# Two weight strips of the next product are loaded and split before the attention half ends, and the strips' buffers become two stores of two

## The chip, the core and the metric

The kernel runs on one core of a Trainium2 chip. A core has a matrix engine (TensorE, "PE" in the rows below; its weight loads are a row of their own, "PEld"), a vector engine (VectorE, "DVE"), a scalar engine (ScalarE, "ACT"), a general engine (GpSimd, "POOL") and a queue engine that here only issues loads (SyncE, "SP"). Each works through its own list of instructions, and they wait for each other by semaphores. The metric is the time of one execution on the device in microseconds, the median of several.

## What is computed

Two layers of an encoder over 256 tokens of width 2048, in float32. Cut to what matters:

```python
for l in range(2):
    u = rmsnorm(x, norm_mix[l])
    proj = u @ w_in[l]                       # 2048 x 8256: queries, keys, values, gates
    y_a = mla_attention(...) @ w_o_mla[l]    # 8 heads, 1024 x 2048
    y_b = neighbourhood_attention(...) @ w_o_na[l]
    merged = sigmoid(gate_a) * y_a + sigmoid(gate_b) * y_b
    x = x + merged @ w_out[l]                # 2048 x 2048
    h = rmsnorm(x, norm_mlp[l]) @ w_ff1[l]   # 2048 x 8192
    x = x + square(relu(h)) @ w_ff2[l]       # 8192 x 2048
return rmsnorm(x, norm_final)
```

## The kernel before

**Products in three pieces.** A float32 number is split into a rounded part `hi` and a remainder `lo`, and a product is made of three matmuls: hi times hi, lo of the activations times hi of the weights, hi of the activations times lo of the weights. So every piece of weights goes through three steps: a load into a buffer `raw` (1 MB, three such buffers, issued by SP), a cast by ACT that makes `hi`, and a subtraction by DVE that makes `lo`. These are the lines L176 and L177 in `parts` for the large products, and L197 and L198 in `weights` for the others. A matmul (L537) takes one 128 x 128 block of the activations as stationary operand (from a tile called `pair`) and 512 columns of a `hi` or `lo` strip as moving operand; it adds into one of eight PSUM banks.

**Two halves of a layer.** The attention half (half A) makes the projections, the two attentions and their output products; the last of them multiplies by `w_o_mla`, in four column blocks (`for c4 in range(4)`, matmuls at L306 and L310). Behind each block `merge` (L902, L903) gates and adds the two attention results, and `turned` (transposes at L605, splits at L165 and L169) turns the sum into stationary tiles for the next product. The second half (half B) makes the product by `w_out` and then the MLP, all with `gemm_s`.

**gemm_s.** One call makes 1024 columns of a product over 2048 rows. It goes through eight double rows of weights in the order 0, 4, 1, 5, 2, 6, 3, 7. Three of them are in `pairs` and are done with one level of Strassen's scheme, which needs seven block products in place of eight: DVE first makes four sums of weight blocks (L574, L577, L578), then `cut` splits 1536 columns of the raw weights and 2048 columns of sums. The other five double rows are split whole (2048 columns, a "whole strip"). At the end the eight banks are combined (L587 on ACT, L586 on DVE) and handed to `evac`. For `w_out` this adds to the residual (L936) and starts `turned_pair`: transposes (L507), a scaled copy by ACT (L926 behind `w_out`, L980 behind `w_ff1`), sums of activations (L473 to L476), a cast by ACT (L516) and a subtraction by DVE (L517).

**Buffers.** Half A and half B hold pools of their own, opened and closed at the border. In half B the split strips lie in `wpool2` with four buffers for `hi` and four for `lo`; each holds up to 2048 columns, and a new strip takes one of the four that has come free. In half A the pool `wpool` holds strips of 1024 columns, and `tmp` holds the temporaries of the attention heads.

**Order.** The program is written as if in one stream; generators started with a lag (`start`, advanced by `tick` after every few matmuls) put transposes and splits between the matmuls. A scheduler then sets the order of the instructions on each engine, going by costs of its own. On the chip each engine keeps to that order: a cast that stands behind another one on ACT waits for it, even when its own data is there.

Of the kernel before, what the change touches and what calls it, by code (L numbers as in the profile page):

```python
# [39 lines left out]
P = 128  # L40
# [35 lines left out]
def trunk(ctx: ExitStack, tc: tile.TileContext, x, x_turned, w_in, w_uq, w_ukv, rpb, w_o_mla, w_o_na,  # L76
# [7 lines left out]

    tmp = wpool = None
    hbufs, smalls, strips = HBUFS, SMALL, False

    def bank():
        return psum.tile([P, 512], F32, tag="bank", name="bank", bufs=8)
# [81 lines left out]

    def parts(src):

        lo, hi = (wpool.tile([P, 2048 if strips else 1024], F32R, tag=tag, name=tag,
                             bufs=hbufs)[:, :src.shape[-1]] for tag in ("lo", "hi"))
        nc.scalar.copy(hi, src)  # L176
        nc.vector.tensor_tensor(lo, src, hi.bitcast(F32), op=ALU.subtract)  # L177
        return hi, lo
# [342 lines left out]
        return  # L521
        yield

    def gemm_s(w, c0, get, order, pairs, evac):

# [17 lines left out]
            for i, ah, al, wh, wl in todo:  # L545
                mm(i, ah, wl)

        def cut(src):
            out, step = [], 2048 if strips else 1024
            for c in range(0, src.shape[-1], step):  # L550
                hi, lo = parts(src[:, c:min(c + step, src.shape[-1])])
                out += [(hi[:, i:i + 512], lo[:, i:i + 512]) for i in range(0, hi.shape[-1], 512)]
            return out

        first = next(j for j in order if j in pairs)
        for j in order:
            raw = raws.tile([P, 2048], F32, tag="raw", name="raw", bufs=RBUFS)
            nc.sync.dma_start(raw.rearrange("p (k n) -> p k n", n=1024),
                              w[2 * j * P:(2 * j + 2) * P, c0:c0 + 1024].rearrange("(k p) n -> p k n", p=P))
            if j not in pairs:  # L560
                ws = cut(raw)
                ah, al = get(j)
                products(*((i, ah[2 * k + t], al[2 * k + t], *ws[2 * k + side])
                           for k in range(2) for i, t, side in ((2, 0, 1), (3, 0, 0), (4, 1, 1), (8, 1, 0))))
                continue
            if j == first:
                drain()
            if strips:
                whole_ts = wpool.tile([P, 2048], F32, tag="sums", name="sums", bufs=1)
                ts = whole_ts[:, :1024], whole_ts[:, 1024:]  # L570
            else:
                ts = [tmp.tile([P, 1024], F32, tag="pp", name="sums", bufs=2) for _ in range(2)]
            t1, t3, t2, t4 = (s[:, i:i + 512] for s in ts for i in range(0, 1024, 512))
            nc.vector.tensor_tensor(ts[0].rearrange("p (a n) -> p a n", a=2),  # L574
                                    raw[:, :512].rearrange("p (a n) -> p a n", a=1).to_broadcast([P, 2, 512]),
                                    raw[:, 512:1536].rearrange("p (a n) -> p a n", a=2), op=ALU.subtract)
            nc.vector.tensor_tensor(t2, raw[:, 1024:1536], t1, op=ALU.subtract)  # L577
            final = nc.vector.tensor_tensor(t4, raw[:, 1536:], t2, op=ALU.subtract)  # L578
            with tc.issue_after(final.ins):
                w11, w22, w21 = cut(raw[:, 512:])  # L580
            w1, w3, w2, w4 = cut(whole_ts) if strips else cut(ts[0]) + cut(ts[1])
            (a11, _, a12, a22, s1, s2, s3, s4), (l11, _, l12, l22, r1, r2, r3, r4) = get(j)
            products((1, a11, l11, *w11), (2, a12, l12, *w21), (3, s4, r4, *w22), (5, s1, r1, *w1),
                     (7, s3, r3, *w3), (6, s2, r2, *w2), (4, a22, l22, *w4))
# [167 lines left out]
    for l in range(DEPTH):  # L752
        half_a = ExitStack()
        hbufs, smalls, strips = HBUFS, SMALL, False
        wpool = half_a.enter_context(tc.tile_pool(name="wpool", bufs=4, reuse_waits="tile"))
        tmp = half_a.enter_context(tc.tile_pool(name="tmp", bufs=2, reuse_waits="tile"))
        wi = w_in[l]
        mix = norm

# [136 lines left out]
        local(2)  # L896
        local(3)
        mg, ms4, mf4 = [None] * NC, [None] * (NC // 2), [None] * (NC // 2)
        for c4 in range(4):
            def merge(t, ps):  # L900
                m, h = part[t, c4], other[t, c4]
                nc.vector.scalar_tensor_tensor(h, h, 1.0, ps, op0=ALU.add, op1=ALU.mult)  # L902
                nc.vector.tensor_tensor(m, m, h, op=ALU.add)  # L903
                if t == 1:
                    start(turned(lambda t, c4=c4: part[t, c4], c4, mg, lambda c: 0.5, mf4, MERGED), 4)

            gemm_a(w_o_mla[l], c4 * 512, att, merge)
            if c4 == 2:
                start(forms(mf4, MERGED, ms4), 4)
        half_a.close()  # L910


        last = l == DEPTH - 1
        half_b = ExitStack()
        strips = True
        wpool = half_b.enter_context(tc.tile_pool(name="wpool2", bufs=4, reuse_waits="tile"))
        tmp = half_b.enter_context(tc.tile_pool(name="tmp2", bufs=2, reuse_waits="tile"))
        mlp = RowNorm()
        xg = [None] * (NC // 2)

# [9 lines left out]
        for g in range(2):  # L930
# [8 lines left out]
                        start(turned_pair(lambda t, c4=c4: xt[t][:, c4 * 512:(c4 + 1) * 512], c, xg, 2 * c4 + c,  # L939
                                          2 * c4 + c in FIRST, gained(2 * c4 + c)), 4)  # L940

            gemm_s(w_out[l], g * 1024, blocks(mg, ms4, MERGED), ORDER, MERGED, residual)
        mlp.scale()

        norm = RowNorm()
# [139 lines left out]
```

## Time and profile before

| | |
|---|---|
| median of three executions | 2600.32 us (2599.18 to 2600.32) |
| profiled execution | 2599.52 us, of which the profile's span is 2597.7 us |
| granted TensorE clock | 0.999 |
| PE busy | 2585.0 us |
| DVE busy | 2176.4 us |
| ACT busy | 1487.5 us |

The profile has a page with one row per engine and groups of instructions by line, and views of the trace: a timeline of one engine (start, duration, engine, line, operation, output and inputs, and in square brackets how long the engine had been idle before and whose work ended that), sums of the waits by what was waited for, and the chain of work that ended last. The rows that carry the argument stand with the prediction.

### The profile page before, as it was taken

How to read it: one execution, taken by the hardware profiler on the slowest of the kernel's cores; microseconds unless marked ns; L12 is line 12 of the kernel's file. 1: busy time of each engine (PE TensorE's matmuls, PEld its weight loads, DVE VectorE, ACT ScalarE, POOL GpSimd, SP SyncE). 2: the span in 40 equal slices, each digit the busy share in tenths (PEclk: the TensorE clock that was granted, in tenths of full speed). 3: DMA queues.
4: the chain of work that ended last, by engine and by line, in shares of the span. 5: the costliest groups of instructions: out<-in, count | busy, mean ns of one | idle time of the engine just before them, and what ended most of it. 6: DMA issues, size and time to landing. Idle time of an engine off the chain costs nothing.

```text
span 2597.7 us, 32260 instructions
## 1 busy us (share of the span) xinstructions
PE 2585.0 (100%) x12432; PEld 2171.9 (84%) x12432; DVE 2176.4 (84%) x2538; ACT 1487.5 (57%) x1732; POOL 98.0 (4%) x118
## 2 busy tenths in 40 slices
PE   9999999999999999999999999999999999999998
PEld 8888889888888888888888888898888888888887
DVE  7778889699988898888667788896999988988885
ACT  6555557456655645546545555574666556555463
POOL 0200000000000010000001000000000000100000
PEclk9999999999999999999999999999999999999999
DMA  7655564555577585675565555645656765856754
GB/s 266 217 171 195 180 205 151 165 191 195 195 219 220 176 259 198 202 239 171 178 201 178 173 194 182 205 149 161 197 180 211 234 199 192 246 194 209 243 180 145
DMA packets 173994, 511.06 MB, mean 197 GB/s; under 512 B 13840, under 2 KB 18832, under 8 KB 173584
## 3 DMA queue, kind: packets, MB, share of 16 engines
q1 hardware_dynamic: 164640, 491.78, 57.1%
q0 software_dynamic: 8768, 16.78, 3.3%
q8 instruction: 97, 1.59, 0.2%
q10 hardware_dynamic: 432, 0.43, 0.1%
q14 instruction: 57, 0.47, 0.1%
HBM read 494.28 MB, written 2.10 MB: 191 GB/s over the span
## 4 chain that ended last, share of the span: by engine, by line
PE 99%; issue 0%; ACT 0%; DVE 0%; POOL 0%; DVEq 0%; POOLq 0%; ACTq 0%
PE bank L537 67%; PE bank L306 8%; PE bank L354 6%; PE bank L310 4%; PE bank L359 3%; PE bank L285 2%; PE bank L507 1%; PE bank L260 1%; PE bank L286 1%; PE bank L314 1%; PE bank L316 1%; PE bank L315 1%; PE bank L258 1%; PE bank L669 1%; PE bank L605 0%
## 5 line engine op out<-in xcount | busy, mean ns | idle before, releaser
L537 PE MATMUL bank<-hi,pair 128*128 128x512 f32 x5124 | 1283.4, 390 | 2.1 <-ACT hi L176 2.1
L537 PEld LDWEIGHTS bank<-hi,pair 128*128 128x128 f32 x5124 | 958.0, 188 | 202.5 <-ACT hi L176 2.9
L176 ACT CAST hi<-raw 128x2048 fp32r<-128x2048 f32 (+3 forms) x416 | 622.7, 1517 | 301.7 <-PE bank L537 165.3
L177 DVE TENSOR_TENSOR lo<-raw,hi 128x2048 fp32r<-128x2048 f32 (+3 forms) x416 | 741.6, 1796 | 63.8 <-ACT hi L176 42.2
L537 PE MATMUL bank<-lo,pair 128*128 128x512 f32 x2562 | 697.2, 390 | 0.0
L537 PEld LDWEIGHTS bank<-lo,pair 128*128 128x128 f32 x2562 | 479.7, 188 | 99.4
L176 ACT CAST hi<-sums 128x2048 fp32r<-128x2048 f32 (+1 forms) x150 | 244.9, 1638 | 297.5 <-DVE sums L578 168.9
L177 DVE TENSOR_TENSOR lo<-sums,hi 128x2048 fp32r<-128x2048 f32 (+1 forms) x150 | 290.7, 1948 | 101.2 <-ACT hi L176 58.2
L198 DVE TENSOR_TENSOR lo<-raw,hi 128x1024 fp32r<-128x1024 f32 (+1 forms) x208 | 248.8, 1201 | 102.9 <-ACT hi L197 99.5
L197 ACT CAST hi<-raw 128x1024 fp32r<-128x1024 f32 (+1 forms) x208 | 214.1, 1035 | 205.0 <-PE bank L306 87.6
L306 PE MATMUL bank<-hi,pair 128*128 128x512 f32 x960 | 245.2, 392 | 0.0
L586 DVE TENSOR_TENSOR wide<-wide,bank 128x512 f32<-128x512 f32 x336 | 214.9, 679 | 6.5 <-PE bank L537 6.4
L306 PEld LDWEIGHTS bank<-hi,pair 128*128 128x128 f32 x960 | 178.3, 188 | 35.8
L354 PE MATMUL bank<-pair,hi 128*128 128x512 f32 x640 | 168.8, 395 | 0.0
L574 DVE TENSOR_TENSOR sums<-raw 128x1024 f32<-128x1024 f32 x126 | 153.7, 1220 | 13.9 <-DMA raw<-in_w_ff 7.3
L310 PE MATMUL bank<-lo,pair 128*128 128x512 f32 x480 | 131.9, 391 | 0.0
L354 PEld LDWEIGHTS bank<-pair,hi 128*128 128x128 f32 x640 | 112.4, 189 | 17.7
L310 PEld LDWEIGHTS bank<-lo,pair 128*128 128x128 f32 x480 | 89.4, 188 | 18.0
L516 ACT CAST pair<-wide 128x512 fp32r<-128x512 f32 x110 | 68.2, 620 | 59.8 <-DVE wide L475 57.5
L359 PEld LDWEIGHTS bank<-pair,lo 128*128 128x128 f32 x640 | 89.4, 190 | 7.2
L359 PE MATMUL bank<-pair,lo 128*128 128x256 f32 x640 | 93.7, 283 | 0.0
L578 DVE TENSOR_TENSOR sums<-raw,sums 128x512 f32<-128x512 f32 x126 | 86.6, 687 | 2.0
(165 smaller groups left out, 1890.7 us busy)
## 6 DMA issues: line engine op xcount, KB each, us to landing
raw<-in_w_ff SPq DMA_DIRECT2D x256, 1024.0 KB, 5.4
raw<-in_w_in SPq DMA_DIRECT2D x120, 1024.0 KB, 5.1
raw<-in_w_out SPq DMA_DIRECT2D x32, 1024.0 KB, 5.6
raw<-in_w_o_na SPq DMA_DIRECT2D x16, 1024.0 KB, 5.0
raw<-in_w_o_mla SPq DMA_DIRECT2D x16, 1024.0 KB, 5.0
xt<-wide POOLq DMA_DIRECT2D x48, 256.0 KB, 5.3
raw<-in_w_in SPq DMA_DIRECT2D x17, 512.0 KB, 5.6
raw<-in_w_ukv SPq DMA_DIRECT2D x8, 1024.0 KB, 5.0
```

Of the source, the lines that this page charges most:

```text
L176: nc.scalar.copy(hi, src)
L177: nc.vector.tensor_tensor(lo, src, hi.bitcast(F32), op=ALU.subtract)
L197: nc.scalar.copy(hi, src)
L198: nc.vector.tensor_tensor(lo, src, hi.bitcast(F32), op=ALU.subtract)
L306: nc.tensor.matmul(ps[t], a, wh[:, k], start=k0 + k + i == 0, stop=False)
L310: nc.tensor.matmul(ps[t], sides(have(acts, k0 + k), t)[0], wl[:, k], start=False, stop=k0 + k == nk - 1)
L354: nc.tensor.matmul(ps[m], wh[:, k, m * P:(m + 1) * P], have(acts, k0 + k), start=k0 + k == 0, stop=False)
L359: nc.tensor.matmul(ps[m][:, :S], wl[:, k, m * P:(m + 1) * P], have(acts, k0 + k)[:, :S], start=False, stop=k0 + k == nk - 1)
L537: nc.tensor.matmul(b[i], x, y, start=count[i] == 1, stop=count[i] == total[i])
L574: nc.vector.tensor_tensor(ts[0].rearrange("p (a n) -> p a n", a=2), raw[:, :512].rearrange("p (a n) -> p a n", a=1).to_broadcast([P, 2, 512]),
L578: final = nc.vector.tensor_tensor(t4, raw[:, 1536:], t2, op=ALU.subtract)
L586: add = lambda o, a, c: nc.vector.tensor_tensor(o, a, c, op=ALU.add)
```

## The change

The pool of the heads' temporaries, `tmp`, gets an exit of its own (`heads_end`). Just before the last column block of `w_o_mla` a new generator `strips_ahead` is started with lag 7. When it runs, it closes `tmp`, opens a pool `wpool3` with two buffers for `hi` and two for `lo`, loads double rows 0 and 4 of `w_out` (the first two in the order, both whole strips) and splits them. `gemm_s` takes them from the dictionary `made` for the first 1024 columns of `w_out`. Half B's own pool `wpool2` shrinks from four buffers to two. The strips then go to the two pools by turns of two, where each pair of `hi` and `lo` made in half B counts as a strip, the two pieces of a Strassen double row too: strips 0 and 1 to the first store, 2 and 3 to the second, 4 and 5 to the first, and so on (`whole_strips[0] // 2 % 2`). So a strip's place is one of two, where it was one of four. What is computed is the same, and so is the number of instructions on each engine. A pool `tmp2` that half B did not use is gone.

```diff
 def parts(src):
-        lo, hi = (wpool.tile([P, 2048 if strips else 1024], F32R, tag=tag, name=tag,
-                             bufs=hbufs)[:, :src.shape[-1]] for tag in ("lo", "hi"))
+        if strips:
+            whole_strips[0] += 1
+        pool, n, bufs = (stores[whole_strips[0] // 2 % 2], 2048, 2) if strips else (wpool, 1024, HBUFS)
+        hi, lo = (pool.tile([P, n], F32R, tag=tag, name=tag, bufs=bufs)[:, :src.shape[-1]] for tag in ("hi", "lo"))
         nc.scalar.copy(hi, src)
         nc.vector.tensor_tensor(lo, src, hi.bitcast(F32), op=ALU.subtract)
         return hi, lo
...
+    def two_rows(w, c0, j):
+        raw = raws.tile([P, 2048], F32, tag="raw", name="raw", bufs=RBUFS)
+        nc.sync.dma_start(raw.rearrange("p (k n) -> p k n", n=1024),
+                          w[2 * j * P:(2 * j + 2) * P, c0:c0 + 1024].rearrange("(k p) n -> p k n", p=P))
+        return raw
...
-    def gemm_s(w, c0, get, order, pairs, evac):
+    def gemm_s(w, c0, get, order, pairs, evac, made={}):
...
-            raw = raws.tile([P, 2048], F32, tag="raw", name="raw", bufs=RBUFS)
-            nc.sync.dma_start(...)
+            raw = None if j in made else two_rows(w, c0, j)
             if j not in pairs:
-                ws = cut(raw)
+                ws = made[j] if j in made else cut(raw)
...
-        tmp = half_a.enter_context(tc.tile_pool(name="tmp", bufs=2, reuse_waits="tile"))
+        heads_end = ExitStack()
+        tmp = heads_end.enter_context(tc.tile_pool(name="tmp", bufs=2, reuse_waits="tile"))
...
+        half_b, made = ExitStack(), {}
+
+        def strips_ahead(l=l, made=made, half_b=half_b, heads_end=heads_end):
+            nonlocal strips
+            heads_end.close()
+            stores[0] = half_b.enter_context(tc.tile_pool(name="wpool3", bufs=2, side="right",
+                                                          reuse_waits="tile"))
+            whole_strips[0] = -1
+            for j in ORDER[:2]:
+                strips = True
+                made[j] = cut(two_rows(w_out[l], 0, j))
+                strips = False
+                if j == ORDER[0]:
+                    stores[0].tile([P, 56], F32, name="phase", bufs=1)
+                yield 1
...
+            if c4 == 3:
+                start(strips_ahead(), 7)
             gemm_a(w_o_mla[l], c4 * 512, att, merge)
...
+        while len(made) < 2:
+            tick()
         half_a.close()
...
-        wpool = half_b.enter_context(tc.tile_pool(name="wpool2", bufs=4, reuse_waits="tile"))
-        tmp = half_b.enter_context(tc.tile_pool(name="tmp2", bufs=2, reuse_waits="tile"))
+        wpool = stores[1] = half_b.enter_context(tc.tile_pool(name="wpool2", bufs=2, reuse_waits="tile"))
...
-            gemm_s(w_out[l], g * 1024, blocks(mg, ms4, MERGED), ORDER, MERGED, residual)
+            gemm_s(w_out[l], g * 1024, blocks(mg, ms4, MERGED), ORDER, MERGED, residual, {} if g else made)
```

How the order of the instructions changes is shown at three places of layer 0; layer 1 has the same rows. A number behind a tile's name tells tiles apart, and the same tile has a number one or a few higher in the new program at times; the lines are a few higher too (L176 and L177 become L179 and L180, L537 becomes L553, L516 becomes L519, L926 becomes L951).

**ACT at the end of the attention half.** `pair_5039` to `pair_5057` are the last block's activations, split behind the last transposes; `hi_5123` and `hi_5177` are the first two whole strips of `w_out`. Before:

```order
L165 ACTIVATE pair_4958<-wide_4955 128x256
L165 ACTIVATE pair_4961<-wide_4955 128x256
L197 CAST hi_5091<-raw_5064 128x1024
L165 ACTIVATE pair_5039<-bank_5034 128x256
L165 ACTIVATE pair_5042<-bank_5034 128x256
L165 ACTIVATE pair_5054<-bank_5049 128x256
L165 ACTIVATE pair_5057<-bank_5049 128x256
L176 CAST hi_5123<-raw_5120 128x2048
L176 CAST hi_5177<-raw_5174 128x2048
```

With the change, where the two strips are called `hi_5093` and `hi_5104`:

```order
L179 CAST hi_5093<-raw_5091 128x2048
L618 ACTIVATE wide_4937<-bank_4932 128x256 x2
L166 ACTIVATE pair_4940<-wide_4937 128x256
L200 CAST hi_5066<-raw_5064 128x1024
L166 ACTIVATE pair_4943<-wide_4937 128x256
L618 ACTIVATE wide_4955<-bank_4950 128x256 x2
L166 ACTIVATE pair_4958<-wide_4955 128x256
L166 ACTIVATE pair_4961<-wide_4955 128x256
L200 CAST hi_5108<-raw_5064 128x1024
L179 CAST hi_5104<-raw_5102 128x2048
L179 CAST hi_5231<-raw_5225 128x1536
L166 ACTIVATE pair_5039<-bank_5034 128x256
```

The two casts of 2048 columns stood behind the four splits of the last activations and stand ahead of them now, between the splits of earlier blocks.

**PE in the first 1024 columns of w_out.** `hi_5235` holds the sums of the first Strassen double row, `hi_5331` is a whole strip. Before:

```order
L537 MATMUL bank_5141<-hi_5331,pair_5160 128x512 x2
L537 MATMUL bank_5129<-hi_5331,pair_5163 128x512 x2
L537 MATMUL bank_5141<-hi_5331,pair_5163 128x512 x2
L537 MATMUL bank_5144<-hi_5331,pair_5163 128x512 x2
L537 MATMUL bank_5238<-hi_5365,pair_4958 128x512
L537 MATMUL bank_5126<-lo_5330,pair_5160 128x512
L537 MATMUL bank_5129<-lo_5330,pair_5160 128x512
L537 MATMUL bank_5251<-hi_5235,pair_5079 128x512
L537 MATMUL bank_5251<-hi_5235,pair_5080 128x512
```

With the change:

```order
L553 MATMUL bank_5249<-hi_5304,pair_5145 128x512
L553 MATMUL bank_5249<-lo_5305,pair_5144 128x512
L553 MATMUL bank_5252<-hi_5235,pair_5079 128x512
L553 MATMUL bank_5252<-hi_5235,pair_5080 128x512
L553 MATMUL bank_5252<-lo_5236,pair_5079 128x512
L553 MATMUL bank_5252<-hi_5304,pair_5144 128x512
L553 MATMUL bank_5252<-hi_5304,pair_5145 128x512
L553 MATMUL bank_5252<-lo_5305,pair_5144 128x512
L553 MATMUL bank_5133<-hi_5331,pair_5167 128x512 x2
L553 MATMUL bank_5136<-hi_5331,pair_5167 128x512 x2
```

`hi_5331` was multiplied while `hi_5235` was still wanted, so they lay in different buffers; now its first product comes after the last product of `hi_5235`, with four other products between them.

**ACT at the start of w_ff1.** `pair_5838` and the later pairs are the last activations of the MLP's input; `hi_6009` and `hi_6074` are sums of Strassen double rows, `hi_6070` is the raw part of the second one, `hi_6036` a whole strip. Before:

```order
L516 CAST pair_5838<-wide_5830 128x512
L424 ACTIVATE junk_5791,sums_5119<-xt1_87 128x512
L176 CAST hi_6009<-sums_6000 128x2048
L176 CAST hi_6036<-raw_6033 128x2048
L516 CAST pair_5842<-wide_5833 128x512
L926 ACTIVATE wide_5869<-bank_5864,g_sb_80 128x256 x2
L516 CAST pair_5872<-wide_5869 128x512
L926 ACTIVATE wide_5885<-bank_5880,g_sb_80 128x256 x2
L516 CAST pair_5893<-wide_5885 128x512
L176 CAST hi_6070<-raw_6063 128x1536
L176 CAST hi_6074<-sums_6065 128x2048
```

With the change:

```order
L519 CAST pair_5839<-wide_5831 128x512
L179 CAST hi_6070<-raw_6064 128x1536
L179 CAST hi_6009<-sums_6001 128x2048
L519 CAST pair_5843<-wide_5834 128x512
L951 ACTIVATE wide_5870<-bank_5865,g_sb_80 128x256 x2
L519 CAST pair_5873<-wide_5870 128x512
L951 ACTIVATE wide_5886<-bank_5881,g_sb_80 128x256 x2
L519 CAST pair_5894<-wide_5886 128x512
L179 CAST hi_6074<-sums_6066 128x2048
L519 CAST pair_5898<-wide_5889 128x512
L951 ACTIVATE wide_5911<-bank_5906,g_sb_80 128x256 x2
L519 CAST pair_5914<-wide_5911 128x512
```

`hi_6070` moved ahead of `hi_6009`, and `hi_6036`, which stood right behind `hi_6009`, is not among these rows any more: it stands two rows after the last of them.

More of the change, by code (lines that the diff above doesn't have):

```diff
@@ L86, in trunk @@
     hbufs, smalls, strips = HBUFS, SMALL, False
+    stores, whole_strips = [None, None], [-1]
     def bank():
@@ L522, in turned_pair, with cut @@
         yield
-    def gemm_s(w, c0, get, order, pairs, evac):
+    def cut(src):
+        out, step = [], 2048 if strips else 1024
+        for c in range(0, src.shape[-1], step):
+            hi, lo = parts(src[:, c:min(c + step, src.shape[-1])])
+            out += [(hi[:, i:i + 512], lo[:, i:i + 512]) for i in range(0, hi.shape[-1], 512)]
+        return out
+    def two_rows(w, c0, j):
[4 more added lines that the diff above has]
+    def gemm_s(w, c0, get, order, pairs, evac, made={}):
         b, count, total = {}, {}, {i: 0 for i in range(1, 9)}
@@ L546, in products @@
                 mm(i, ah, wl)
[L548 to L553, printed above, removed]
         first = next(j for j in order if j in pairs)
         for j in order:
-            raw = raws.tile([P, 2048], F32, tag="raw", name="raw", bufs=RBUFS)
-            nc.sync.dma_start(raw.rearrange("p (k n) -> p k n", n=1024),
-                              w[2 * j * P:(2 * j + 2) * P, c0:c0 + 1024].rearrange("(k p) n -> p k n", p=P))
+            raw = None if j in made else two_rows(w, c0, j)
             if j not in pairs:
-                ws = cut(raw)
+                ws = made[j] if j in made else cut(raw)
                 ah, al = get(j)
@@ L909, in trunk @@
                 start(forms(mf4, MERGED, ms4), 4)
+        while len(made) < 2:
+            tick()
         half_a.close()
         last = l == DEPTH - 1
-        half_b = ExitStack()
         strips = True
-        wpool = half_b.enter_context(tc.tile_pool(name="wpool2", bufs=4, reuse_waits="tile"))
-        tmp = half_b.enter_context(tc.tile_pool(name="tmp2", bufs=2, reuse_waits="tile"))
+        wpool = stores[1] = half_b.enter_context(tc.tile_pool(name="wpool2", bufs=2, reuse_waits="tile"))
         mlp = RowNorm()
```

## The prediction

> **What bounds the kernel now.** I read the page first, then the sums of PE's waits, then the timeline around the border of the two halves.
>
> ```profile
> PE 2585.0 (100%) x12432; PEld 2171.9 (84%) x12432; DVE 2176.4 (84%) x2538; ACT 1487.5 (57%) x1732; POOL 98.0 (4%) x118
> PE 99%; issue 0%; ACT 0%; DVE 0%; POOL 0%; DVEq 0%; POOLq 0%; ACTq 0%
> L537 PE MATMUL bank<-hi,pair 128*128 128x512 f32 x5124 | 1283.4, 390 | 2.1 <-ACT hi L176 2.1
> ```
>
> PE sets the end: 99% of the chain is its own work. A change that removes no matmul can only gain what PE still waits. Those waits, by the view of waits of PE's weight loads:
>
> ```profile
> engine line waited for: us in total, times, longest us
> PEld bank L537 <- ACT hi L176: 2.9, 2, 1.5
> ...
> PEld bank L537 <- ACT pair L516: 0.9, 2, 0.4
> PEld bank L537 <- ACT wide L926: 0.9, 2, 0.4
> ```
>
> The first row is what the change aims at: once per layer PE waits 1.46 us for the cast of a strip. The timeline of layer 0 shows why:
>
> ```profile
> 523.93 0.66 ACT L165 ACTIVATE pair<-bank 128x256 fp32r<-128x256 f32 x2 [0.49 <-DVE pair L169]
> 524.35 0.76 DVE L169 SCALAR_TENSOR_TENSOR pair<-bank,pair 128x256 fp32r<-128x256 f32 x2 [0.45 <-ACT pair L165]
> 525.14 0.39 ACT L165 ACTIVATE pair<-bank 128x256 fp32r<-128x256 f32 x1 [0.55 <-DVE pair L169]
> 525.42 3.71 ACT L176 CAST hi<-raw 128x2048 fp32r<-128x2048 f32 x2
> 527.37 3.52 PEld L537 LDWEIGHTS bank<-hi,pair 128*128 128x128 f32 x16 [1.46 <-ACT hi L176]
> ```
>
> The cast stands on ACT behind four splits that go back and forth with DVE; it starts at 525.42 and PE starts at 527.37. So the most that this change can win here is 2 x 1.46 = 2.9 us, 0.11%. That is less than a measurement of this kernel can tell from no change (about 0.2%, 5.2 us). Everything else depends on whether PE stays as free of waits as it is.
>
> **The change, part by part.** *The gain.* In the new order both casts stand well ahead of the last splits, in a stretch where ACT was idle. Their loads keep their place on SP, so the raw data is there. The wait of 1.46 us goes. I take -1.46 us per layer; it cannot be more, and it is zero only if closing the heads' pool makes the casts wait, which all ended earlier. The shorter pool `tmp2`, the earlier `hi` before `lo` and the helper functions issue nothing and cost nothing.
>
> *The cost.* Half B had four buffers from which a strip took one that was free. Now it has two stores, and a strip must take one of two. A strip that PE holds long (sums of a Strassen double row, whose last products wait for a PSUM bank) now blocks a store although another buffer is free. In the new order this shows as whole strips that are cast later. A whole strip is 24 matmuls of work that needs nothing new from DVE; where it comes later, PE reaches the next Strassen double row sooner, while ACT and DVE have as much to do as before. I worked out each start by hand: from what releases ACT, down the queues of ACT and DVE in their new order, to the product that wants the result. The durations:
>
> ```profile
> L176 ACT CAST hi<-raw 128x2048 fp32r<-128x2048 f32 x186 | 353.5, 1913 | 95.1 <-PE bank L537 62.3 <-DMA raw<-in_w_ff 18.0 <-PE bank L306 8.3
> L176 ACT CAST hi<-raw 128x1536 fp32r<-128x1536 f32 x102 | 151.3, 1483 | 126.6 <-DMA raw<-in_w_ff 62.3 <-PE bank L537 51.1 <-DMA raw<-in_w_out 7.3
> 738.30 4.70 PE L537 MATMUL bank<-hi,pair 128*128 128x512 f32 x20
> 742.84 1.98 PE L537 MATMUL bank<-lo,pair 128*128 128x512 f32 x8
> L507 PE MATMUL bank<-ident,wide 128*128 128x128 f32 x256 | 35.7, 272 | 0.0
> 635.95 0.83 ACT L926 ACTIVATE wide<-bank,g_sb 128x256 f32<-128x256 f32 x2
> 636.81 0.62 ACT L516 CAST pair<-wide 128x512 fp32r<-128x512 f32 x1
> 637.34 0.83 ACT L926 ACTIVATE wide<-bank,g_sb 128x256 f32<-128x256 f32 x2
> ```
>
> Twenty products start in 742.84 - 738.30 = 4.54 us, so one takes 0.227 us of PE, and its result is there 0.39 us after its start (mean of the group on the page). The cast of 2048 columns takes 1.91 us (3.71 - 1.91 = 1.80 where it follows another at once), that of 1536 takes 1.48. A copy and cast of activations takes 637.34 - 635.95 = 1.39 us. I allow 0.05 us for a hand-over between engines, an estimate from the border: 525.42 + 1.91 = 527.33, and PE starts at 527.37.
>
> 1. *First 1024 columns of w_out.* `hi_5331` needs the buffer of `hi_5235`, whose last product comes only five starts before the product that wants `hi_5331`. From one to the other: 0.39 + 0.05 + 1.91 + 0.05 = 2.40 us; PE has 5 x 0.227 = 1.13 us of work. PE waits 1.27 us. Ahead of it the cast `hi_5365` now stands behind `hi_5304` and two splits on ACT: 0.39 + 0.05 + 1.91 + 0.66 + 1.48 + 0.05 = 4.5 us, less 0.1 for each that follows at once, against 17 products, 3.9 us; 0.6 us late. And a PSUM bank is freed by a split on DVE that stands behind the `lo` of `hi_5304` (2.29), two splits (0.76), a weight sum (1.22) and two small sums (0.56): by the same reckoning 0.6 us late. Together 2.5 us; at least 1.3 (the first alone).
>
> 2. *Second 1024 columns.* On ACT the first strip of w_ff1, `hi_5802`, now stands ahead of `hi_5714`, which PE wants first. `hi_5802` waits for a product that PE makes 12 starts before it wants `hi_5714`: 0.39 + 0.05 + 1.91 + 1.80 + 0.05 = 4.20 us against 12 x 0.227 = 2.72. PE waits 1.5 us (at least 1).
>
> 3. *Start of w_ff1.* Here the chain is long. Before, the same work of DVE ran thus:
>
> ```profile
> 633.75 2.29 DVE L177 TENSOR_TENSOR lo<-sums,hi 128x2048 fp32r<-128x2048 f32 x1 [0.71 <-ACT hi L176]
> 635.97 2.28 DVE L177 TENSOR_TENSOR lo<-raw,hi 128x2048 fp32r<-128x2048 f32 x1
> 638.17 0.68 DVE L517 TENSOR_TENSOR pair<-wide,pair 128x512 fp32r<-128x512 f32 x1
> 638.77 1.22 DVE L574 TENSOR_TENSOR sums<-raw 128x1024 f32<-128x1024 f32 x1
> ...
> 642.92 1.75 DVE L177 TENSOR_TENSOR lo<-raw,hi 128x1536 fp32r<-128x1536 f32 x1
> 644.59 0.28 DVE L475 TENSOR_TENSOR wide<-wide 128x128 f32<-128x128 f32 x1
> ```
>
> In the new order the strip of 635.97 (`lo_6035`, now `lo_6037`) is gone from this run, and what is left is 2.22 us (633.75 to 635.97) and 6.42 us (638.17 to 644.59), 8.64 us. It ends with the `lo` of `hi_6070`. Before it, from the last transposes of the input: 0.27 us for a transpose, 1.39 us for the first activations, 1.48 us for `hi_6070`, which now stands in front, and 1.91 us for `hi_6009`, 5.05 us. With two hand-overs the chain is 13.8 us. PE has 34 products between those transposes and the first that wants the result, 7.7 us. It waits 6.1 us, spread over `hi_6009` and what follows. Behind it the next cast of activations stands after `hi_6074` on ACT and comes 0.8 late, and its `lo` 0.3. Together 7.2 us. What waited here before goes into it:
>
> ```profile
> 636.10 0.19 PEld L537 LDWEIGHTS bank<-hi,pair 128*128 128x128 f32 x1 [0.45 <-ACT pair L516]
> 636.83 0.30 PEld L537 LDWEIGHTS bank<-hi,pair 128*128 128x128 f32 x2 [0.44 <-ACT wide L926]
> ```
>
> That is 0.89 us, so the term is +6.3 us. It is at least 0.4: without queues, `hi_6009` and its `lo` take 0.39 + 0.05 + 1.91 + 0.05 + 2.29 + 0.05 = 4.7 us from the product that frees the buffer, and PE has 15 products (3.4 us) meanwhile, which leaves 1.3 less 0.9. It is at most about 7.
>
> 4. *Starts of w_ff2*, four per layer. The same move: the whole strip is cast after the next Strassen double row instead of ahead of it. The chain is the cast of sums (0.39 + 0.05 + 1.91 + 0.05), then DVE's run of the rows above with one L517 in front of the sums in place of two, 8.64 - 0.6 = 8.0 us, and 0.05: 10.5 in all. In the first block PE has 42 products meanwhile (9.5 us), in the other three 47 (10.7 us). So 1.0 us and nothing; behind it a cast of activations and its `lo` come about 0.9 and 0.2 late each time. I take 2.1 us for the first and 1.0 for each of the others, 5.1 us per layer; at least nothing, at most 9 (PE's next strips start later than I have them).
>
> In the rest of half B every cast in the new order is released at least 12 products (2.7 us) before its use, so I add nothing there. POOL and SP keep their order.
>
> **The sum** per layer: -1.46 + 2.5 + 1.5 + 6.3 + 5.1 = +13.9 us; two layers +27.9. Against the profiled execution, 2599.52 us (1.8 us over its span), that is 2627.4; the median of the runs is 0.8 above the profiled one, so **2628 us**. From the lower bounds: -1.46 + 1.3 + 1.0 + 0.4 + 0 = +1.2 per layer, 2603 us. From the upper: -1.46 + 2.5 + 1.5 + 7 + 9 = +18.5, 2637 us.
>
> **Rivals.** *Only the short ways count.* DVE and ACT may run ahead of my bookkeeping, since I start it late and give each queue its full length; then only the waits for a buffer stay: 2603 to 2612. For it: PE waited nowhere else in half B before, so the old order had room that I can't read from a wait. Against: at these places PE itself releases ACT, and a lead is lost there.
>
> *No new wait at all.* The two strips cast early put ACT two casts (3.7 us by the row of 525.42) ahead at the start of half B. If that lead holds, every later cast is early, the moved ones are covered, and only the gain stays: 2600.3 - 2.9 = 2597.4, no change that can be measured. It decides at the first use of `hi_5331`: with a lead there would be no wait. Against it: that cast cannot start before PE has made the last product of `hi_5235`, and a lead of ACT does not move PE. A gain over 0.2% would need more than all waits of half B, 2.9 + 0.9 + 0.9 = 4.7 us.
>
> *The casts stay late.* If the new pool has to wait for heads that end late, the old wait of 1.46 stays and the costs come on top: 2631.
>
> *The clock drops.*
>
> ```profile
> PEclk9999999999999999999999999999999999999999
> core 0: 2597.7 us, clock 0.999
> ```
>
> In the trace before, the longest wait in half B is 1.46 us and the granted clock stays full. I expect single waits up to about 2.6 us, and about 6 us of them within 15. If PE then ran those 34 products of term 3 at half its clock, they would take 7.7 us more per layer, part of it in place of the waits; at most 2628 + 15.4 = 2643. The Trainium skill, page "TensorE: Matmul & The Clock Gate", section "What's actually happening", has the matrix engine fall to half its clock after an idle window of about 3.4 us. By that rule none of my waits is quite long enough; no row of this trace tests it.
>
> **Chances.** My sum, give or take its bounds, 2612 to 2640: 0.72. Only the short ways: 0.13, three quarters of it beyond 2605.5. No new wait: 0.08. The casts stay late: 0.03. The clock drops: 0.02. Faster by more than 0.2%: 0.02. Slower is 0.72 + 0.10 + 0.03 + 0.02 = 0.87, same 0.08 + 0.03 = 0.11, faster 0.02. The range goes from 2605, just above the lower bounds, to 2638.
>
> **What would show it.** In the new profile the row "PEld bank L537 <- ACT hi L176" (then L553 and L179) loses its two waits of 1.46 us at the border, and gains waits of 1.3 to 1.5 us in w_out, about 6 us around the start of w_ff1, mostly for `lo` of DVE, and about 1 us for a cast of activations at each start of w_ff2. PE's busy time stays near 2585 us as a sum of products. I am wrong if the border still has its wait, or if PE goes through w_out and the start of w_ff1 without idle time of a us or more.

## The result, and the profile after

| | before | after |
|---|---|---|
| median | 2599.89 us (2599.18 to 2600.32) | 2630.59 us (2628.37 to 2631.80) |
| profile's span | 2597.7 us | 2628.3 us |
| granted TensorE clock | 0.999 | 0.998 |
| PE busy | 2585.0 us | 2599.3 us |

The ratio is 1.0117, with a 95% interval of 1.0100 to 1.0135: slower by 30.7 us. The forecast was 2628. (One execution of a kernel further down, the one with a table of turns, took 7529.13 us, with 128x512 products of 894 ns where 390 ns is usual and a granted clock of 1.000; why is not known, and it is in none of the comparisons.)

The page of the changed kernel: busy time by engine, the chain that ended last, and the group of products with `hi`.

```profile
PE 2599.3 (99%) x12432; PEld 2170.5 (83%) x12432; DVE 2181.0 (83%) x2538; ACT 1488.3 (57%) x1732; POOL 91.8 (3%) x118
...
PE 91%; DVE 4%; ACT 3%; issue 1%; DMA 1%; DVEq 0%; ACTq 0%; POOLq 0%; POOL 0%; SPq 0%
...
L553 PE MATMUL bank<-hi,pair 128*128 128x512 f32 x5124 | 1286.4, 392 | 11.6 <-ACT hi L179 6.4
```

The chain was 99% PE; now 8% of it runs over DVE, ACT and DMA, which had 0% of it before. The sums of PE's waits say for what (by weight loads; total, times, longest):

```profile
PEld bank L553 <- ACT hi L179: 9.7, 8, 1.7
PEld bank L553 <- DVE lo L180: 8.7, 6, 2.9
PEld bank L553 <- ACT pair L519: 7.1, 12, 0.7
PEld bank L553 <- DVE pair L520: 5.5, 13, 0.5
PEld bank L553 <- ACT wide L951: 2.4, 6, 0.5
PEld bank L553 <- issue: 1.7, 2, 0.9
PEld bank L553 <- ACT wide L1005: 1.6, 8, 0.2
```

These are 36.7 us in 55 waits (one more, of 0.2 us, is left out), where there were 4.7 us in 6. None of them is at the border. There the timeline of PE's weight loads, around the place where the old kernel waited 1.46 us, has no bracket:

```profile
525.64 0.81 PEld L612 LDWEIGHTS bank<-ident,wide 128*128 128x128 f32 x6
526.42 3.49 PEld L553 LDWEIGHTS bank<-hi,pair 128*128 128x128 f32 x16
```

So the change does what it says, and the loss lies behind it. The larger waits of layer 0, from the same timeline (`w_out` at 550 to 609, the start of `w_ff1` at 638 to 650, of the first block of `w_ff2` at 739):

```profile
550.63 0.30 PEld L553 LDWEIGHTS bank<-hi,pair 128*128 128x128 f32 x2 [0.77 <-ACT hi L179]
553.64 0.30 PEld L553 LDWEIGHTS bank<-hi,pair 128*128 128x128 f32 x2 [0.86 <-issue]
556.41 3.50 PEld L553 LDWEIGHTS bank<-hi,pair 128*128 128x128 f32 x16 [1.55 <-ACT hi L179]
...
608.41 5.31 PEld L553 LDWEIGHTS bank<-hi,pair 128*128 128x128 f32 x24 [1.41 <-ACT hi L179]
...
640.83 0.30 PEld L553 LDWEIGHTS bank<-hi,pair 128*128 128x128 f32 x2 [1.69 <-ACT hi L179]
...
649.57 0.19 PEld L553 LDWEIGHTS bank<-lo,pair 128*128 128x128 f32 x1 [2.89 <-DVE lo L180]
...
739.72 0.19 PEld L553 LDWEIGHTS bank<-lo,pair 128*128 128x128 f32 x1 [1.28 <-DVE lo L180]
```

How much of the loss is layer 0's is read from one copy on ACT that stands at the same place of both programs, in the attention half of layer 1. Before and after:

```profile
1534.21 0.57 ACT L587 COPY wide<-bank 128x512 f32<-128x512 f32 x1
```

```profile
1550.84 0.57 ACT L594 COPY wide<-bank 128x512 f32<-128x512 f32 x1
```

Up to there the change costs 16.6 us, which is layer 0 (0.4 of it is there already at 241 us, from a wait at the start of the program), and layer 1 costs the other 30.6 - 16.6 = 14.0. Here 30.6 is the difference of the two spans.

### The profile page after: what moved, and what is told of

It reads as the page before. It is cut to its first block, busy times and chain, and to the rows that moved or that the text cites. A ratio compares the mean times of both kernels' runs of the same rounds, so it can differ in the third digit from the quotient of the medians.

```text
span 2628.3 us, 32241 instructions
## 1 busy us (share of the span) xinstructions
PE 2599.3 (99%) x12432; PEld 2170.5 (83%) x12432; DVE 2181.0 (83%) x2538; ACT 1488.3 (57%) x1732; POOL 91.8 (3%) x118
## 4 chain that ended last, share of the span: by engine, by line
PE 91%; DVE 4%; ACT 3%; issue 1%; DMA 1%; DVEq 0%; ACTq 0%; POOLq 0%; POOL 0%; SPq 0%
PE bank L553 60%; PE bank L309 8%; PE bank L357 6%; PE bank L313 4%; PE bank L362 3%; ACT hi L179 2%; PE bank L288 2%; DVE lo L180 1%; PE bank L510 1%; PE bank L263 1%; PE bank L289 1%; PE bank L317 1%; PE bank L319 1%; PE bank L318 1%; DVE sums L581 1%
## 5 line engine op out<-in xcount | busy, mean ns | idle before, releaser
L553 PE MATMUL bank<-hi,pair 128*128 128x512 f32 x5124 | 1286.4, 392 | 11.6 <-ACT hi L179 6.4
L553 PEld LDWEIGHTS bank<-hi,pair 128*128 128x128 f32 x5124 | 956.0, 188 | 224.0 <-ACT hi L179 9.7
L179 ACT CAST hi<-raw 128x2048 fp32r<-128x2048 f32 (+3 forms) x416 | 624.1, 1517 | 433.0 <-PE bank L553 303.1
L180 DVE TENSOR_TENSOR lo<-raw,hi 128x2048 fp32r<-128x2048 f32 (+3 forms) x416 | 743.1, 1798 | 85.4 <-ACT hi L179 67.0
L553 PE MATMUL bank<-lo,pair 128*128 128x512 f32 x2562 | 690.7, 391 | 6.4 <-DVE lo L180 6.4
L553 PEld LDWEIGHTS bank<-lo,pair 128*128 128x128 f32 x2562 | 480.7, 188 | 109.1 <-DVE lo L180 8.7
L180 DVE TENSOR_TENSOR lo<-sums,hi 128x2048 fp32r<-128x2048 f32 (+1 forms) x150 | 290.8, 1949 | 102.6 <-PE bank L553 55.9
L179 ACT CAST hi<-sums 128x2048 fp32r<-128x2048 f32 (+1 forms) x150 | 244.8, 1637 | 229.6 <-DVE sums L585 119.8
L585 DVE TENSOR_TENSOR sums<-raw,sums 128x512 f32<-128x512 f32 x126 | 86.8, 689 | 2.0
L584 DVE TENSOR_TENSOR sums<-raw,sums 128x512 f32<-128x512 f32 x126 | 86.5, 687 | 1.0
```

The costliest lines, as they stand in the source:

```text
L553: nc.tensor.matmul(b[i], x, y, start=count[i] == 1, stop=count[i] == total[i])
```

## Experiments

All are compared with runs of the kernel before on the same chip, whose median was 2599.5 to 2599.8 us. My theory was that the two stores, each strip bound to one of them, cost time, and the early casts cost nothing. The rivals were that the early casts cost, and that any split of four buffers costs. A third, called "scatter" in two of the expectations, is that any other layout of the memory makes the scheduler write another order, and that this costs at random.

### The stores alone

The kernel before, with only this; nothing in the text is cast early:

```diff
-        lo, hi = (wpool.tile([P, 2048 if strips else 1024], F32R, tag=tag, name=tag,
-                             bufs=hbufs)[:, :src.shape[-1]] for tag in ("lo", "hi"))
+        if strips:
+            whole_strips[0] += 1
+        pool, n, bufs = (stores[whole_strips[0] // 2 % 2], 2048, 2) if strips else (wpool, 1024, hbufs)
...
-        wpool = half_b.enter_context(tc.tile_pool(name="wpool2", bufs=4, reuse_waits="tile"))
+        wpool = stores[1] = half_b.enter_context(tc.tile_pool(name="wpool2", bufs=2, reuse_waits="tile"))
+        stores[0] = half_b.enter_context(tc.tile_pool(name="wpool3", bufs=2, reuse_waits="tile"))
```

> The kernel before with one thing taken from the change: the four buffers of half B become two stores of two, by turns of two. The program text loads nothing early; the strips are cut inside gemm_s as before. Theory 'stores' (a strip that must take one of two places waits for a strip that is held long): all of the cost is here, 2630 us (2626 to 2634), because the order of instructions on every engine comes out the same as with the whole change. Theory 'early' (the strips cut early push other work aside): 2600 us, as before.

Measured: 2630.08 us (2629.16 to 2630.86), ratio 1.0117 (1.0103 to 1.0130), the whole loss. Its waits:

```profile
PEld bank L540 <- ACT hi L179: 10.9, 8, 1.7
PEld bank L540 <- DVE lo L180: 8.1, 9, 2.9
```

The order of the instructions is the same as in the changed kernel, on every engine, as the expectation has it, although nothing in this text is cast early. By the addresses, the new store lies where the heads' temporaries lay, so its first buffers are free earlier than those of half A's strips, and the scheduler puts the two casts ahead of the border by itself. The text that starts them early adds nothing. Both the gain and the loss come from the stores.

### The same, strip by strip in turn

One operator less: `whole_strips[0] % 2` in place of `whole_strips[0] // 2 % 2`.

> The kernel before with only the two stores of two, as in the run with the stores alone, except that the strips take them one by one in turn (odd strips the one, even strips the other) and not two by two. Theory 'the turn decides': two strips that follow each other, one of them sums of a double row that PE holds long, no longer lie in the same store. By the same reckoning from the order as in the prediction, the waits for a buffer fall from 4.4 us per layer (1.5 + 0.8 for the sums at the start of w_ff1, 1.5 + 0.6 in w_out) to 0.7 (three of 0.1 to 0.35 us), and PE waits at no place longer than about 1 us; with the border wait gone (-1.46 per layer) and up to 3 us per layer of small ones, 2601 us (2598 to 2607), and no stretch at half clock. Rival 'any two stores cost': the loss comes from splitting four buffers in two, whichever way the turns go, or from casts put ahead of the border; then it stays at 2620 us or above, with 5 us or more of waits at the start of w_ff1.

Measured: 2600.56 us (2600.31 to 2601.61, ten runs), ratio 1.0003 (0.9994 to 1.0013), no difference that can be measured. What is left of the waits for strips:

```profile
PEld bank L540 <- ACT hi L179: 2.6, 10, 0.5
PEld bank L540 <- DVE lo L180: 1.6, 2, 0.8
```

So it isn't the split into two stores, and not the early casts, which are in this order too. It is the turn of two. A pool hands out whichever of its two buffers is free, but of two strips that follow each other into one store, the second has to take the buffer that the first left. The first term shows it: by the addresses in the program, `hi_5331` took the place of `hi_5235`, whose last product comes five starts ahead. ACT in the changed kernel, where the cast is released by PE and PE goes on at 556.41 (554.45 + 1.91 = 556.36):

```profile
554.45 3.71 ACT L179 CAST hi<-raw 128x2048 fp32r<-128x2048 f32 x2 [2.38 <-PE bank L553]
```

With turns of one, the same strip takes the place of the raw part of a Strassen double row, whose last product comes 13 starts ahead, 13 x 0.227 = 2.95 us, more than the 2.40 us that the way needs (10.6 starts). The same count over all 386 `hi` strips of half B gives at least 14 starts in the kernel before, 5, 8 and 10 once per layer each with turns of two, and at least 10 with turns of one.

This is what a buffer forces by itself, 4.4 us per layer by the reckoning in the expectation above. The rest of the loss comes through the order on ACT and DVE, which the scheduler makes anew for each layout: no run here changes the places and keeps the order.

### The whole change, with turns of one

```diff
-        pool, n, bufs = (stores[whole_strips[0] // 2 % 2], 2048, 2) if strips else (wpool, 1024, HBUFS)
+        pool, n, bufs = (stores[whole_strips[0] > 1 and whole_strips[0] % 2], 2048, 2) if strips else (wpool, 1024, HBUFS)
```

> The whole change with one thing edited: from the fourth strip of half B on, the strips take the two stores one by one in turn (the first three lie in the new store, the others alternate), not two by two. Theory 'the turn decides': as in the run with stores alone and turns of one (2600.6), the waits for a buffer fall from 4.4 to 0.7 us per layer, and nothing of the early casts is lost: 2600 us (2598 to 2604), at the border no wait, at the start of w_ff1 about 2 us per layer. Rival 'the early casts themselves cost' (they are in the text here, not left to the scheduler): 2605 or more.

Measured: 2600.24 us (2600.01 to 2600.62, eleven runs), ratio 1.0002 (0.9993 to 1.0011). The early casts in the text cost nothing. But they win nothing either: the border's 2.9 us are gone, and small waits stand in their place, most of them at the start of `w_ff1` (2.5 of 2.9 us in layer 0):

```profile
PEld bank L553 <- ACT hi L179: 1.7, 8, 0.4
PEld bank L553 <- DVE lo L180: 1.6, 2, 0.8
PEld bank L553 <- ACT pair L519: 1.3, 2, 0.7
PEld bank L553 <- ACT wide L951: 1.1, 2, 0.6
```

That is 5.7 us, against 4.7 before.

### Four stores of one

The kernel before with `stores[whole_strips[0] % 4]`, one buffer of `hi` and one of `lo` in each: no choice at all.

> As the kernel with the stores alone, but four stores of one buffer each, by turns, so that a strip has no choice at all. Theory 'stores': less choice costs at least as much as a choice of two. At the starts of w_ff2 hi comes 10 starts after its buffer is free (it was 12 with two stores), which is 0.4 us worse in eight places; the first wait in w_out is smaller. I expect 2632 us (2624 to 2645). Theory 'scatter': no relation with the number of stores, 2600 to 2630.

Measured: 2627.11 us (2625.51 to 2628.98), ratio 1.0106 (1.0092 to 1.0119). A fixed rotation costs about as much as the turn of two, but at other places: 3.16 us for the first `hi` at the border (shown below, with the clock), and in layer 1 waits of 1.9 and 2.0 us in `w_out` where layer 0 has 0.6 and none. The value lies in the range of both theories, so this run does not tell "stores" from "scatter".

### The places of the kernel before

The whole change, but each strip goes to the store that holds the place it had before, by a list for each layer (195 digits, one for each strip):

```diff
-        pool, n, bufs = (stores[whole_strips[0] // 2 % 2], 2048, 2) if strips else (wpool, 1024, HBUFS)
+        pool, n, bufs = (stores[int(places[whole_strips[0]])], 2048, 2) if strips else (wpool, 1024, HBUFS)
```

> The whole change, but a strip's store is not set by turns of two: a list of 195 places per layer names for each strip the store that holds the buffer which its hi took in the kernel before. Two stores of two and the early strips stay. Theory 'stores': nearly all of the cost goes, since hi is hardly held up; lo has to follow hi's store, and two products per layer still want hi 10 starts after its buffer comes free (0.35 us short each, some more by queues): 2600 us (2597 to 2606). Theory 'early': 2628 us.

Measured: 2602.06 us (2601.44 to 2603.83, ten runs), ratio 1.0010 (1.0001 to 1.0019), as expected: the cost is the choice of places. The two longest waits that are left, each once per layer, are these in layer 0:

```profile
550.81 1.92 PEld L557 LDWEIGHTS bank<-hi,pair 128*128 128x128 f32 x9 [1.19 <-ACT hi L183]
...
636.65 0.30 PEld L557 LDWEIGHTS bank<-hi,pair 128*128 128x128 f32 x2 [0.99 <-ACT hi L183]
```

### A list for hi and another for lo: a miss

`lo` lay in other places than `hi` before, so the next kernel has two lists, and comes closer still to the places of before.

> The whole change, but the two stores are no longer taken by turns: each strip's hi and lo go, each by a list of its own, to the place that the kernel before gave them. Theory 'only the choice of the place costs': with both lists as before, what is left is the border's gain of 1.46 us per layer less 0.35 + 0.35 + 0.14 us for buffers and what follows from them, 2600 us (2597 to 2603), at least as fast as the run that took one list for both (2602.1). Rival 'the early casts themselves cost' (ACT and DVE do the two strips while they are wanted for the last product of the attention half, or the strips hold two buffers longer): no better than 2602, with waits left at the start of w_ff1 of 2 us or more per layer.

Measured: 2609.33 us (2608.45 to 2609.82), ratio 1.0036 (1.0023 to 1.0048), 7 us slower than with one list. Neither theory has this. The new waits lie at two places of each layer. The first is in the second 1024 columns of `w_ff1`; ACT first, then PE's weight loads:

```profile
690.35 1.91 ACT L186 CAST hi<-raw 128x2048 fp32r<-128x2048 f32 x1 [5.13 <-DMA raw<-in_w_ff]
692.17 1.89 ACT L186 CAST hi<-sums 128x2048 fp32r<-128x2048 f32 x1
...
694.11 5.34 PEld L560 LDWEIGHTS bank<-hi,pair 128*128 128x128 f32 x24 [1.36 <-ACT hi L186]
```

The cast of sums, for which PE waits, stands behind a cast of raw weights whose load lands only at 690.3; ACT has been idle for 5.13 us. In the run with one list the scheduler put the sums first and the two casts of raw weights behind them, and PE waits for no strip there. The second place is the start of `w_ff2`, 2.4 us between 724 and 730 us, of which 1.51 for activations that DVE splits behind two `lo`; how it came about was not followed up. So a place changes the time in two ways: by the buffer that a cast waits for, and by the order that the scheduler makes of it. I had reckoned with the first alone.

### A table of turns: another miss

The whole change with a store for each of the eleven strips of a product, chosen so that the long waits for buffers go:

```diff
+        plan[:] = [f ^ c for c in (0, 0, 1, 1, 0, 0, 1, 0, 0, 0, 0)]
+        first_store[0] = 1 - f
```

> The whole change, but the order of the turns is swapped or not for each of the eleven products of half B (a table of eleven bits), so that the two long waits at the start of w_ff1 and those in w_out go. Theory 'the turn decides': the waits for a buffer by the order are 0.35 us in w_out, 0.57 in w_ff1 and three of 0.63 at the starts of w_ff2, 2.8 us per layer instead of 4.4, and no longer together in one place; with what they pull behind them up to 6 us per layer, less 1.46: 2606 us (2601 to 2612), with no wait above 2 us and no stretch at half clock. Rival 'any two stores cost': 2620 or above.

Measured: ratio 1.0087 (1.0072 to 1.0102), 2620 to 2624 us (three executions). The value of the rival came, though the theory behind it is refuted by the turns of one. Where the time goes is read from one more execution:

> The kernel with the table of eleven bits once more, for a profile that shows where its 24 us go: 2620 to 2624 us. Theory 'the order on ACT and DVE carries it': the scheduler has set the casts in yet another order, and one or two places hold most of the loss, in which a cast that PE wants stands behind a cast or a difference that waits for something later (a load, or a product further on), though the buffers alone cost 2.8 us per layer. Rival 'many small waits': no place above 2 us, the loss spread over the starts of all products.

Measured: 2621.73 us. It is many small waits:

```profile
PEld bank L559 <- ACT hi L185: 15.9, 23, 1.2
PEld bank L559 <- DVE lo L186: 13.6, 16, 1.0
```

I had 0.57 us in `w_ff1` and three waits of 0.63 us per layer in `w_ff2`; from 820 us on, the timeline of layer 0 has thirteen of 0.4 to 1.0 us, mostly two at a time, and ten of them in the later blocks of `w_ff1`. The reckoning by buffers alone gave 2.8 us per layer, and the two rows come to 29.5 / 2 = 14.8. So what it leaves out is the larger part. As I read it, that is a `hi` that is late and makes its `lo` late, and the queues behind both; this was not shown.

### hi in a pool of its own: a miss

The kernel before with `hi` in a pool of four that lies over the heads' temporaries, and `lo` in a pool of four over half A's strips; every strip keeps its choice of four:

```diff
-        lo, hi = (wpool.tile([P, 2048 if strips else 1024], F32R, tag=tag, name=tag,
-                             bufs=hbufs)[:, :src.shape[-1]] for tag in ("lo", "hi"))
+        hi, lo = ((hpool if strips and tag == "hi" else wpool).tile(
+            [P, 2048 if strips else 1024], F32R, tag=tag, name=tag, bufs=hbufs)[:, :src.shape[-1]] for tag in ("hi", "lo"))
...
-        tmp = half_b.enter_context(tc.tile_pool(name="tmp2", bufs=2, reuse_waits="tile"))
+        hpool = half_b.enter_context(tc.tile_pool(name="hpool", bufs=4, reuse_waits="tile"))
```

> The kernel before with the hi strips of half B in a pool of their own with four buffers, which lies where the heads' temporaries lay, and the lo strips in another with four. A strip keeps its choice of four places, and the first two casts can stand ahead of the last splits as in the change. Theory 'stores': the gain without the cost; the border's wait of 1.46 us goes in both layers and nothing comes in w_out or w_ff2, so 2597 us (2595 to 2599), with the waits at the start of w_ff1 about as before. Theory 'early' : about 2628 us. Theory 'scatter' (any other pool makes the scheduler write another order, and that costs at random): anything from 2600 to 2630.

Measured: 2610.34 us (2608.15 to 2614.99), ratio 1.0043 (1.0029 to 1.0057). The border's wait for `hi` is gone, and the same strip's `lo` takes its place a few microseconds later; then come two waits at the start of `w_ff1`:

```profile
531.61 1.69 PEld L537 LDWEIGHTS bank<-lo,pair 128*128 128x128 f32 x8 [1.84 <-DVE lo L177]
...
637.82 0.30 PEld L537 LDWEIGHTS bank<-lo,pair 128*128 128x128 f32 x2 [2.08 <-DVE lo L177]
...
640.40 0.29 PEld L537 LDWEIGHTS bank<-hi,pair 128*128 128x128 f32 x1 [1.83 <-ACT pair L516]
```

The `lo` at the border lies over half A's strips, which PE uses up to the border, and it stands on DVE behind the last gates (L902), which end at 529.3: freeing `hi` alone only moves the wait. The other two hang on the order on DVE and ACT again; which move of it made them was not followed up.

## Why the prediction was right, point by point

**The gain.** -1.46 us per layer, as said; the border has no wait.

**Why stores cost.** Right, and shown: the stores alone make the whole loss, turns of one undo it. The prediction put it down to "one of two where it was one of four". That was too coarse, since turns of one also leave one of two; what decides between turns of two and of one is that the second strip of a turn is left no choice, shown at `hi_5331`. How much more comes on top through the order is not foretold by the buffers: three layouts that have at least 9 starts for every `hi` (the table of turns, the two lists, `hi` apart) cost 10 to 24 us all the same. "Scatter" is not refuted as an account of those three.

**The terms.** The brackets of weight loads add up to more than the time lost, as a load runs ahead of its product where nothing waits (the one at 645.70 by 0.23 us) and hardly behind a wait (the one at 649.57 by 0.01): 32.0 us of waits came on top (36.7 less 4.7), while the span grew by 30.6, of which 0.4 is the start and 3.4 products at a lower clock (below), so 26.8. Over 49 more waits that is 0.11 us too much in each. This is fitted to the span, so the table tests how the loss is spread, and not its total. With 0.1 taken off each wait, layer 0 compares so:

| term | brackets, number | less 0.1 each | predicted |
|---|---|---|---|
| 1, first 1024 columns of `w_out` | 3.18, 3 | 2.9 | 2.5 |
| 2, second 1024 | 1.88, 2 | 1.7 | 1.5 |
| 3, start of `w_ff1` | 8.13, 11 | 7.0 | 7.2 |
| 4, first start of `w_ff2` | 2.60, 4 | 2.2 | 2.1 |
| 4, the three others | 4.0, 9 | 3.1 | 3.0 |

Less what waited there before (1.4 and 0.7), the sum is 14.8; layer 0 measured 16.3 without the start, or 14.6 without the clock, and the prediction 13.9. In layer 1 it is 14.0, or 12.3: there the wait at 649.57 has a counterpart of 2.16 us instead of 2.89, and the one at 739.72 has none.

*Term 1* had 1.3 us for `hi_5331` and 0.6 each for `hi_5365` and a PSUM bank; three waits came, of 1.55, 0.77 and 0.86 us.

*Term 2* went by the letter in layer 0 (in layer 1 most of it stands as a wait of 1.62 us for a `lo`). ACT casts a whole strip ahead of the sums that PE wants first, and PE starts as the second cast ends (608.36):

```profile
604.65 1.92 ACT L179 CAST hi<-raw 128x2048 fp32r<-128x2048 f32 x1 [1.01 <-PE bank L553]
606.47 1.89 ACT L179 CAST hi<-sums 128x2048 fp32r<-128x2048 f32 x1
```

*Term 3* was a chain of 13.8 us from the last transposes to the end of the `lo` of `hi_6070`, 8.64 of it DVE's run. ACT and DVE in the new trace:

```profile
636.11 0.84 ACT L951 ACTIVATE wide<-bank,g_sb 128x256 f32<-128x256 f32 x2 [1.97 <-PE bank L510]
...
638.88 1.89 ACT L179 CAST hi<-sums 128x2048 fp32r<-128x2048 f32 x1
```

```profile
640.81 2.29 DVE L180 TENSOR_TENSOR lo<-sums,hi 128x2048 fp32r<-128x2048 f32 x1 [1.96 <-ACT hi L179]
...
647.76 1.76 DVE L180 TENSOR_TENSOR lo<-raw,hi 128x1536 fp32r<-128x1536 f32 x1
```

DVE's run is 649.52 - 640.81 = 8.71 us, and with a transpose ahead of 636.11 the chain is 13.7. The wait of 2.89 us at 649.57 is the end of it. One sign was wrong: the waits around the start of `w_ff1` are not mostly for `lo`, which has 0.31 + 2.89 = 3.2 of the 8.1 us; 1.7 are for a `hi` and the rest for activations.

**The clock.** This is where a step failed. The rival "the clock drops" had a chance of 0.02, on the argument that no single wait would be long enough. The longest wait was 2.89 us where up to about 2.6 was foreseen, and the clock fell once in each layer. Granted clock (third figure from the right) in windows at the start of `w_ff1`, layer 0:

```profile
644.00:650.00 6.00, 3.42 (x13) 1.00 0.00 0
650.00:652.00 2.00, 1.65 (x5) 0.73 0.71 150
652.00:654.00 2.00, 2.00 (x6) 0.50 0.90 371
654.00:656.00 2.00, 2.00 (x10) 0.92 0.04 12
```

The products lose 2 x (0.27 + 0.50 + 0.08) = 1.7 us by it per layer, 3.4 in all, but not all of that is lost time. In layer 1 the clock falls ahead of the long wait for `lo`; ACT behind the last transposes, and PE's weight load at the end of the wait:

```profile
1945.29 0.84 ACT L951 ACTIVATE wide<-bank,g_sb 128x256 f32<-128x256 f32 x2 [0.83 <-PE bank L510]
...
1958.76 0.19 PEld L553 LDWEIGHTS bank<-lo,pair 128*128 128x128 f32 x1 [2.16 <-DVE lo L180]
```

From the one to the other it is 13.47 us, and 649.57 - 636.11 = 13.46 in layer 0, where the clock falls behind this wait. So in layer 1 the slow products only took the place of waiting, and the clock adds at most 1.7 us, in layer 0. The distance between forecast and result is 2.7 us (30.6 of span against 27.9): at most 1.7 the clock, 0.4 the start, and about 0.6 the terms. The rival's price of 7.7 us per layer was too high, as the half clock held for about 3.4 us and not for all 34 products, and its argument from the length of single waits does not hold (last section).

**PE's busy time** was to stay near 2585 us and came to 2599.3. Of the 14.3 us, 3.4 are the clock. For the rest, a product counts as busy until its result is there, about 0.39 us, and so covers a part of each wait behind it: the wait of 2.89 us of the weight load is 2.58 in the row of its product. Busy time of PE is no measure of work to half a per cent.

**The other rivals.** "Only the short ways" (2603 to 2612), "no new wait" and "the casts stay late" did not come, for the reasons given against them: PE itself releases ACT at these places, and no lead of ACT helps. Turns of one come nearest to "no new wait"; they measured 2600.2 rather than 2597.4, since 3.9 us of small waits came where 2.9 went.

## What to carry to other kernels

A pool that hands out any free buffer does work that a fixed rotation doesn't: when buffers are split, look whether each tile still has a choice when the buffer it would take is held long, and try turns of one before turns of two. Where a scheduler sets the order, a change of memory is a change of order too; waits for buffers worked out by hand say which places to look at, but a run has to say what the queues make of them. And a wait of 1.46 us per layer, in a kernel whose matrix engine is 99% of the chain, was never worth more than 0.11%: none of the eight variants run here was measurably faster.

## What was not expected of the hardware

The TensorE clock was halved after waits much shorter than I thought it needed, and not always after the same ones. In layer 1 of the changed kernel the last waits ahead of the drop are 1.69 and 0.55 us, the same as at 640.83 and 642.08 in layer 0, where the clock stayed full until after the wait of 2.89:

```profile
1950.01 0.30 PEld L553 LDWEIGHTS bank<-hi,pair 128*128 128x128 f32 x2 [1.69 <-ACT hi L179]
1951.27 0.41 PEld L553 LDWEIGHTS bank<-hi,pair 128*128 128x128 f32 x2 [0.55 <-ACT wide L951]
```

In the kernel with `hi` in its own pool, the single waits of 1.84 us (at 531.61) and 2.28 (its counterpart in layer 1) left the clock full, while 2.08 and 1.83 close together brought 3.4 us at half clock in layer 1 and twice that in layer 0. With four stores, one wait of 3.16 us was enough:

```profile
529.23 4.88 PEld L540 LDWEIGHTS bank<-hi,pair 128*128 128x128 f32 x15 [3.16 <-ACT hi L179]
```

```profile
530.00:532.00 2.00, 2.00 (x6) 0.50 0.85 350
```

And in the kernel with the table, 29.5 us of waits, none above 1.2, didn't move it (the last few microseconds of the program, behind the last product, show about half clock in every kernel, the one before included).

What decides can be read from the traces. Where a run has several drops, they lie whole multiples of 3.41 us apart (1951.39 - 650.91 = 1300.48 us, 381 times 3.413, in the changed kernel), so a run can be cut into stretches of 3.41 us that end at its drops. PE's busy time (second figure) and clock of the stretch ahead of the drop, for layer 0, and then for layer 1 with the stretch behind it:

```profile
647.50:650.91 3.41, 0.98 (x3) 1.00 0.16 25
```

```profile
1947.98:1951.39 3.41, 1.92 (x8) 1.00 0.61 250
1951.39:1954.80 3.41, 3.41 (x9) 0.50 0.01 2
```

Over the ten kernels, ten drops stand ahead of the end, and each follows a stretch in which PE was busy for 0.65 to 1.92 of the 3.41 us. Of the stretches at full clock that no drop follows (from 20 us on), the least busy have 1.80 (one, right behind a half clock, in the kernel with the stores alone), 1.93 and 1.99. So by these figures it is not the length of a wait but how little PE is busy, under about 1.9 us, within one stretch of a fixed grid; the same group of waits does it or not by where the grid cuts it. The Trainium skill, page "TensorE: Matmul & The Clock Gate", section "What's actually happening", has the clock drop after an idle window of about 3.4 us, and come back after a busy one of the same length, in windows that run freely. The length of the half clock in the changed kernel (1.7 us lost, so 3.4 us at half) agrees, and so does a drop that comes once and not the other time; the idle that it took does not, as no wait there reached 3.4 us, none ahead of the drop in layer 1 was above 1.69, and PE was busy for 1.92 us of the stretch ahead of it.
